# A decoder layer's SwiGLU in two phases: seven products in place of eight, and a down projection summed in PSUM

## The chip, the core and the metric

The kernel runs on one core of a Trainium2 chip. The metric is the device time of one launch in microseconds; before the change it is 1984.45 us, the median of three runs (1980.93 to 1986.12). TensorE (PE) multiplies matrices, VectorE (DVE), ScalarE (ACT) and GpSimd (POOL) do elementwise work, and SyncE (SP) issues the DMAs.

## The reference

One step of a hybrid decoder layer for 1024 prompt tokens and 8 x 8 sample tokens that share the weights: a conv branch and a sparse-attention branch, merged by gates, an output projection, and a SwiGLU FFN. The change touches the last part (D_MODEL 1024, D_FF 2816):

```python
def back(x, f, u_out, o, p):
    nsa = o.reshape(B, T, Q_W) @ p['w_nsa_o']
    mix = (f['g_conv'] * u_out + f['g_nsa'] * nsa) @ p['w_out']
    x = x + f['g1'] * mix
    h = rms_norm(x, p['ffn_norm_g']) * (1.0 + f['sc2']) + f['sh2']
    ffn = (jax.nn.silu(h @ p['w_gate']) * (h @ p['w_up'])) @ p['w_down']
    return x + f['g2'] * ffn
```

## The kernel before, in words

All is float32. A product is made of float32r matmuls: each operand is split into a high part (a copy to float32r on ScalarE, `acopy`, line 152) and a low part (source minus high, on VectorE or GpSimd), and `mm3` (lines 338 to 340) adds high x high, high x low and low x high in PSUM. `mm2` (343, 344) takes sample rows whose high and low parts lie side by side in one operand. `sub_sb` (158) alternates between VectorE and GpSimd.

Until about 1020 us the kernel computes norms, qkv, both branches and the attention; the change leaves this as it is. What follows:

- Merging (lines 1484 to 1508). For each of 8 blocks m of 128 channels and 3 chunks of tokens (`CH`: 384, 384, 320, the last with the 64 sample tokens) it loads two saved arrays from DRAM (`tn`, `mc`, five buffers), multiplies with `w_nsa_o`, and writes the merged rows as high and low parts `mh_`, `ml_`, one tile per chunk. w_out comes by 512 KB loads of 128 columns each; four of the eight run here, four later through `fr`.
- Projection (`out_half`, `norm2`). `out_half(i, j)` multiplies token tile i (eight of 128 tokens, the ninth is the samples) with half j of w_out, 24 matmuls of 512 columns, scales the sum by the gate (line 1601) and adds it to `x1[i]` (1602), which stays in SBUF. After the second half it computes the mean square and a scaled copy `xn` (1611 to 1613). `norm2` transposes `xn` on TensorE, applies the adaLN scale and shift (1580) and writes the high and low parts back into `mh_`, `ml_`, the FFN's inputs.
- FFN (`up_tile`, `down`). For each of 22 tiles of 128 of the 2816 hidden channels: 512 KB each of w_gate and w_up, split; per chunk 24 matmuls for gate and 24 for up; sigmoid and two multiplications (1663 to 1665), and the result split into `acth`, `actl`. After every second tile `down` loads two tiles of w_down, and for each token tile and half of the output sums the two tiles' products in PSUM (2 x 3 matmuls of 512 columns), scales them (1701) and adds them to `x1` (1702). The last `down` stores.

The order of instructions on every engine is set by a planner, which simulates the program and on each engine takes the ready instruction that stands first in program order; a later instruction can so be put ahead of one whose operands aren't ready. At run time each queue is in order. A tile of a pool has a fixed number of buffers (`bufs`): a new tile with the same tag waits until the oldest is released, and a pool opened after another was closed may lie in its memory and wait for its tiles.

Of the kernel before, what the change touches and what calls it, by code (L numbers as in the profile page):

```python
# [19 lines left out]
D = 1024  # L20
# [103 lines left out]
def emit(tc, I, O):  # L124
# [1345 lines left out]
    mh_ = [T(mp, [128, 8, 384], f"mh{c}", F32R) for c in range(3)]  # L1470
    ml_ = [T(mp, [128, 8, w], f"ml{c}", F32R) for c, (_, w) in enumerate(CH)]
    woS = ExitStack()
    wop = mkpool(woS, "wo", side="right")
    with ExitStack() as es:
        cp2 = mkpool(es, "c1")
        wo = [[T(wop, [128, 8, 512], f"wo{e}{j}", F32R) for e in "hl"] for j in range(2)]
        wov = I["w_out"].rearrange("(k p) c -> p k c", p=128)

        def load_wo(m, raw):

            last[0] = nc.sync.dma_start(raw, wov[:, :, m * 128:m * 128 + 128])
            hi, lo = (t[:, :, m % 4 * 128:m % 4 * 128 + 128] for t in wo[m // 4])
            acopy(hi, raw)
            (V if WOE[m] == 'V' else G).tensor_tensor(lo, raw, f(hi), op=ALU.subtract)

        for m in range(8):
# [3 lines left out]
            if m in WOM:  # L1490
                load_wo(WOM.index(m), T(cp2, [128, 8, 128], "woraw", bufs=2))
            if w_:
                two = T(pss, [128, 2, 512], "pS", bufs=2)
            for c in (1, 2, 0):
                c0, w = CH[c]
                tn = T(cp2, [128, 384], "tn", bufs=5)
                mc = T(cp2, [128, 384], "mc2", bufs=5)
                nc.sync.dma_start(tn[:, :w], th_d[8 + m][:, c0:c0 + w])
                nc.sync.dma_start(mc[:, :w], mc_d[m][:, c0:c0 + w])
                if w_:  # L1500
                    pn[m, c] = nsa(two[:, c - 1, :w] if c else T(ps, [128, 512], "pT", bufs=3)[:, :w], w_, c)
                V.scalar_tensor_tensor(tn[:, :w], tn[:, :w], 1.0, pn.pop((m, c)), op0=ALU.add, op1=ALU.mult)
                V.tensor_tensor(tn[:, :w], tn[:, :w], mc[:, :w], op=ALU.add)
                acopy(mh_[c][:, m, :w], tn[:, :w])
                n = min(w, TP - c0)
                G.tensor_tensor(ml_[c][:, m, :n], tn[:, :n], f(mh_[c][:, m, :n]), op=ALU.subtract)
                if n < w:
                    G.tensor_tensor(mh_[c][:, m, w:], tn[:, n:w], f(mh_[c][:, m, n:w]), op=ALU.subtract)
# [3 lines left out]
    gp = mkpool(top, "gp")  # L1512
    x1p = mkpool(top, "x1")
    x1 = [T(x1p, [128, D], f"x1_{i}") for i in range(9)]

    def gates(i, out, pool, tag, bufs, ps):
        gm = T(pool, [128, 8, 128], tag, bufs=bufs).rearrange("p a b -> p (a b)")[:19]
        nc.sync.dma_start(gm, g_d[i])
        for ind, n in (("indgp", 128), ("indgs", 128)):
            g_ = T(gp, [n, D], ind)  # L1520
            out.append(g_)
            for j in range(2):
                pg_ = T(ps, [128, 512], "pt", bufs=4)
                PE.matmul(pg_[:n], C(ind)[:19], gm[:, j * 512:j * 512 + 512], start=True, stop=True)
                acopy(g_[:, j * 512:j * 512 + 512], pg_[:n], 1.0 if i else 0.5)
                yield

    def load_up(t, pool):

        for nm in ("w_gate", "w_up"):  # L1530
            raw = T(fr, [128, 8, 128], "w", bufs=3)
            nc.sync.dma_start(raw, I[nm][:, t * 128:t * 128 + 128].rearrange("(k p) c -> p k c", p=128))
            first = t == 0 and nm == "w_gate"
            hi, lo = (T(fr if first else pool(), [128, 8, 128], "w" if first else f"w{e}", F32R, bufs=3) for e in "hl")
            acopy(hi, raw)
            sub_sb(lo, raw, f(hi))
            yield hi, lo


    h2h, h2l = mh_, ml_  # L1540
# [3 lines left out]
    c2S = ExitStack()  # L1544
    cp2 = mkpool(c2S, "c2")
    ssq2 = T(cp2, [128, 9], "ssq2")
    rs2 = T(cp2, [128, 9], "rs2")
    G1, G2 = [], []
    for _ in gates(0, G1, cp2, "xn", 2, psf):
        pass  # L1550

    def load_x1(i):
        n = 128 if i < 8 else 64
        nc.sync.dma_start(x1[i][:n], I["x_prompt"][i * 128:(i + 1) * 128] if i < 8 else I["x_sample"])

    for i in range(2):
        load_x1(i)
    for m in range(len(WOM), 8):
        load_wo(m, T(fr, [128, 8, 128], "w", bufs=3))
    with tc.issue_after(getattr(last[0], "ins", last[0])):  # L1560
        for i in range(2, 9):
            load_x1(i)
    G.memset(x1[8][64:128], 0.0)
    fwp = []
    ld0 = load_up(0, lambda: fwp[0])
    wgu = [next(ld0)]

    xns = {}

    def norm2(tiles):  # L1570
        c, o = tiles[0] // 3, tiles[0] % 3 * 128
        n = 64 if tiles[0] == 8 else 128
        w = n * len(tiles)
        for k in range(8):
            pt = T(psf, [128, 512], "pt", bufs=4)
            for j, i in enumerate(tiles):
                PE.transpose(pt[:, j * 128:j * 128 + n], xns[i][:n, k * 128:(k + 1) * 128], ident[:n, :n])
            hf = T(cp2, [128, 384], "hf2", bufs=2)
            if n == 128:
                V.tensor_scalar(hf[:, :w], pt[:, :w], A2[:, k, 0:1], B2[:, k, 0:1], op0=ALU.mult, op1=ALU.add)  # L1580
            else:
                hs_ = hf[:, :64].rearrange("p (b t) -> p b t", b=8)
                V.tensor_tensor(hs_, pt[:, :64].rearrange("p (b t) -> p b t", b=8), bc(A2[:, k, 1:9], 2, 8), op=ALU.mult)
                V.tensor_tensor(hs_, hs_, bc(B2[:, k, 1:9], 2, 8), op=ALU.add)
            acopy(h2h[c][:, k, o:o + w], hf[:, :w])
            sub_sb(h2l[c][:, k, o:o + w], hf[:, :w], f(h2h[c][:, k, o:o + w]))

    def out_half(i, j):
        n = 128 if i < 8 else 64
        c, o = i // 3, i % 3 * 128  # L1590
        gx = G1[i == 8]
        p = T(psf, [128, 512], "pf", bufs=4)
        for k in range(8):
            w_ = [wo[j][e][:, k, :] for e in range(2)]
            if i < 8:
                mm3(p, mh_[c][:, k, o:o + n], ml_[c][:, k, o:o + n], *w_, k == 0, k == 7)
            else:
                mm2(p, mh_[2][:, k, 256:384], *w_, k == 0, k == 7)
        tmp = T(cp2, [128, 512], "xt", bufs=2)
        xj = x1[i][:, j * 512:j * 512 + 512]  # L1600
        V.tensor_tensor(tmp, p, gx[:, j * 512:j * 512 + 512], op=ALU.mult)
        V.tensor_tensor(xj[:n], xj[:n], tmp[:n], op=ALU.add)
        if i == 8:

            lo = T(cp2, [64, 512], "xt", bufs=2)
            acopy(lo, tmp[64:128])
            V.tensor_tensor(xj[:n], xj[:n], lo, op=ALU.add)
        if j == 0:
            return
        xn = T(cp2, [128, D], "xn", bufs=2)  # L1610
        S.activation(xn[:n], x1[i][:n], AF.Square, accum_out=ssq2[:n, i:i + 1])
        rsqrt_mean(rs2[:n, i:i + 1], ssq2[:n, i:i + 1], D, 1)
        V.tensor_scalar(xn[:n], x1[i][:n], rs2[:n, i:i + 1], None, op0=ALU.mult)
        xns[i] = xn

    for i in range(3):
        out_half(i, 0)
    for tiles in ((0, 1), (2,), (3, 4), (5,), (6, 7)):
        for i in tiles:
            if i > 2:  # L1620
                out_half(i, 0)
            out_half(i, 1)
        norm2(tiles)
    for j in range(2):
        out_half(8, j)
    woS.close()


    with ExitStack() as es:
        fw = mkpool(es, "fw", side="right")  # L1630

        fwp.append(fw)
        fa = mkpool(es, "fa", side="right")
        wgu.append(next(ld0))
        norm2((8,))
        c2S.close()
        fb = mkpool(es, "fb", side="right")
        NF = FF // 128
        acts, wds = {}, {}

        def up_tile(t):
            wg, wu = wgu if t == 0 else load_up(t, lambda: fw)
            ah = T(fa, [128, TP + 128], "acth", F32R, bufs=3)
            al = T(fa, [128, TP], "actl", F32R, bufs=3)
            p = {}

            def product(j, c):
                p[j, c] = T(psf, [128, 512], "pf", bufs=4)
                fm(p[j, c][:, :CH[c][1]], (wg, wu)[j], (h2h[c], h2l[c]), 8, 0, CH[c][1])

            if t == 0:

                for c in range(2):
                    product(0, c)
            for c, (c0, w) in enumerate(CH):
                if (0, c) not in p:
                    product(0, c)
                product(1, c)
                pg_, pu_ = p[0, c], p[1, c]
                if t in (1, 2):  # L1660
                    next(g2, None)
                sg_ = T(fa, [128, 384], "sg", bufs=2)
                S.activation(sg_[:, :w], pg_[:, :w], AF.Sigmoid)  # L1663
                V.tensor_tensor(sg_[:, :w], sg_[:, :w], pg_[:, :w], op=ALU.mult)  # L1664
                V.tensor_tensor(sg_[:, :w], sg_[:, :w], pu_[:, :w], op=ALU.mult)  # L1665
                acopy(ah[:, c0:c0 + w], sg_[:, :w])
                n = min(w, TP - c0)
# [111 lines left out]
```

## Time and profile before

| | |
|---|---|
| median of three runs | 1984.45 us |
| the profiled execution | 1986.18 us |
| its span, first to last instruction | 1984.4 us |
| TensorE busy | 1901.3 us (96%) |
| VectorE busy | 1328.0 us (67%) |
| ScalarE, GpSimd busy | 716.6, 759.6 us |
| mean granted TensorE clock | 0.982 |
| DMA | 191.37 MB, 96 GB/s over the span |

Busy is the share of the span in which an engine has at least one instruction under way. A matmul's record holds its time through the array, so that records of successive matmuls overlap; how fast they follow each other is read from their starts. An idle time is put down to what ended it. The clock is in shares of full speed (2.4 GHz); 0.5 is the lower of its two levels, 1.2 GHz.

### The profile page before, as it was taken

How to read it: one execution, taken by the hardware profiler on the slowest of the kernel's cores; microseconds unless marked ns; L12 is line 12 of the kernel's file. 1: busy time of each engine (PE TensorE's matmuls, PEld its weight loads, DVE VectorE, ACT ScalarE, POOL GpSimd, SP SyncE). 2: the span in 40 equal slices, each digit the busy share in tenths (PEclk: the TensorE clock that was granted, in tenths of full speed). 3: DMA queues.
4: the chain of work that ended last, by engine and by line, in shares of the span. 5: the costliest groups of instructions: out<-in, count | busy, mean ns of one | idle time of the engine just before them, and what ended most of it. 6: DMA issues, size and time to landing. Idle time of an engine off the chain costs nothing.

```text
span 1984.4 us, 29719 instructions
## 1 busy us (share of the span) xinstructions
PE 1901.3 (96%) x11036; PEld 1707.7 (86%) x11036; DVE 1328.0 (67%) x2217; ACT 716.6 (36%) x1711; POOL 759.6 (38%) x737
## 2 busy tenths in 40 slices
PE   8987999999999699999998999999999999999998
PEld 3887998898898598888877889899999999999997
DVE  4778799969969667888865563535634644653655
ACT  5435632445444326777843233121121111112110
POOL 3888401256346475654545224121121121121213
PEclk9999999999999899999999999999999999999999
DMA  9586444445534442100036302111121111111102
GB/s 314 165 250 216 143 123 139 143 123 161 157 129 143 131 150 102 48 19 1 7 105 205 101 11 76 54 49 48 33 64 32 43 54 33 43 54 43 43 11 91
DMA packets 170823, 191.37 MB, mean 96 GB/s; under 512 B 13847, under 2 KB 135719, under 8 KB 170606
## 3 DMA queue, kind: packets, MB, share of 16 engines
q1 hardware_dynamic: 161462, 155.91, 25.5%
q0 software_dynamic: 9216, 33.56, 5.1%
q8 instruction: 87, 1.43, 0.3%
q14 instruction: 58, 0.48, 0.1%
HBM read 163.65 MB, written 30.27 MB: 98 GB/s over the span
## 4 chain that ended last, share of the span: by engine, by line
PE 55%; DVE 2%; issue 1%; DMA 1%; ACT 0%; POOL 0%; SPq 0%; DVEq 0%; POOLq 0%; ACTq 0%
PE pf L338 10%; PE pf L340 10%; PE pf L339 10%; PE pt L340 4%; PE pt L339 4%; PE pt L338 4%; PE pT L1400 3%; PE po L1407 2%; PE po L1408 2%; PE pS L1359 1%; PE pS L1361 1%; PE pS L1364 1%; DVE x L1702 0%; PE pt L343 0%; PE pt L344 0%
## 5 line engine op out<-in xcount | busy, mean ns | idle before, releaser
L338 PE MATMUL pf<-mh,wh 128*128 128x384 f32 (+1 forms) x1032 | 336.7, 326 | 0.0
L340 PE MATMUL pf<-mh,wl 128*128 128x384 f32 (+1 forms) x1032 | 336.5, 326 | 0.0
L339 PE MATMUL pf<-ml,wh 128*128 128x384 f32 (+1 forms) x1032 | 336.5, 326 | 0.0
L1668 POOL TENSOR_TENSOR actl<-sg,acth 128x384 fp32r<-128x384 f32 (+1 forms) x66 | 66.4, 1005 | 488.9 <-ACT acth L152 488.9
L338 PEld LDWEIGHTS pf<-mh,wh 128*128 128x128 f32 x1032 | 193.7, 188 | 7.3 <-DVE sg L1665 3.0
L340 PEld LDWEIGHTS pf<-mh,wl 128*128 128x128 f32 x1032 | 193.7, 188 | 4.0
L339 PEld LDWEIGHTS pf<-ml,wh 128*128 128x128 f32 x1032 | 193.7, 188 | 3.2
L338 PE MATMUL pd<-hh,whi 128*128 128x384 f32 (+1 forms) x576 | 193.5, 336 | 1.0 <-ACT stg L152 0.9
L340 PE MATMUL pd<-hh,wlo 128*128 128x384 f32 (+1 forms) x576 | 191.6, 333 | 0.8 <-DVE wlo L270 0.8
L339 PE MATMUL pd<-hl,whi 128*128 128x384 f32 (+1 forms) x576 | 191.5, 332 | 0.0
L1096 DVE SCALAR_TENSOR_TENSOR y<-U,wdT,y 128x1024 f32<-128x1024 f32 x120 | 161.9, 1349 | 0.6
L1702 DVE TENSOR_TENSOR x<-x,dt 128x512 f32<-128x512 f32 x180 | 146.3, 813 | 5.4
L340 PE MATMUL pt<-wdh,actl 128*128 128x512 f32 x352 | 139.0, 395 | 0.0
L339 PE MATMUL pt<-wdl,acth 128*128 128x512 f32 x352 | 138.5, 393 | 0.0
L1663 ACT ACTIVATE sg<-pf 128x384 f32<-128x384 f32 (+1 forms) x66 | 30.8, 467 | 295.1 <-PE pf L340 291.8
L338 PE MATMUL pt<-wdh,acth 128*128 128x512 f32 x352 | 137.1, 389 | 0.0
L1664 DVE TENSOR_TENSOR sg<-sg,pf 128x384 f32<-128x384 f32 (+1 forms) x66 | 34.9, 528 | 146.4 <-ACT sg L1663 146.4
L1701 DVE TENSOR_TENSOR dt<-pt,indgp 128x512 f32<-128x512 f32 x160 | 110.7, 692 | 25.9 <-PE pt L340 10.9
L958 POOL TENSOR_TENSOR vv<-kraw,vv 128x256 fp32r<-128x256 f32 x80 | 92.0, 1175 | 66.1 <-ACT vv L152 65.9
L338 PEld LDWEIGHTS pd<-hh,whi 128*128 128x128 f32 x576 | 109.6, 190 | 7.7 <-ACT stg L152 1.2
L1388 POOL TENSOR_SCALAR P<-P,ast 128x640 f32<-128x640 f32 (+7 forms) x128 | 89.1, 723 | 70.0 <-DVE ast L1384 68.1
L152 ACT ACTIVATE whi<-wraw 128x512 fp32r<-128x512 f32 (+1 forms) x133 | 81.7, 626 | 92.4 <-PE pd L339 41.2
(493 smaller groups left out, 4920.5 us busy)
## 6 DMA issues: line engine op xcount, KB each, us to landing
wraw<-in_w_in SPq DMA_DIRECT2D x68, 256.0 KB
wraw<-in_w_ada SPq DMA_DIRECT2D x64, 256.0 KB
w<-in_w_gate SPq DMA_DIRECT2D x22, 512.0 KB
w<-in_w_up SPq DMA_DIRECT2D x22, 512.0 KB
w<-in_w_down SPq DMA_DIRECT2D x22, 512.0 KB
x<-in_x_prompt SPq DMA_DIRECT2D x16, 512.0 KB
araw<-in_w_ada SPq DMA_DIRECT2D x32, 256.0 KB
th_d<-th SPq DMA_DIRECT2D x32, 192.0 KB
```

What stands on the lines that cost most here:

```text
L152: S.activation(out, in_, AF.Copy, scale=scale)
L338: PE.matmul(out, ah, bh, start=first, stop=False)
L339: PE.matmul(out, ah, bl, start=False, stop=False)
L340: PE.matmul(out, al, bh, start=False, stop=last)
L958: G.tensor_tensor(vv[:, :, 1], r, f(vv[:, :, 0]), op=ALU.subtract)
L1096: V.scalar_tensor_tensor(op, U[:, k:k + TP], wk, op, op0=ALU.mult, op1=ALU.add)
L1388: G.tensor_scalar(P_[br][g][:, :w], P_[br][g][:, :w], st[:, 2, br, g:g + 1], 1.0, op0=ALU.mult, op1=ALU.mult)
L1400: PE.transpose(pT[:nk, g * 128:(g + 1) * 128], a, ident)
L1407: PE.matmul(po, va, ph[:nk], start=(bi == 0), stop=False)
L1668: G.tensor_tensor(al[:, c0:c0 + n], sg_[:, :n], f(ah[:, c0:c0 + n]), op=ALU.subtract)
L1701: V.tensor_tensor(tmp, p, gx[:, cs_], op=ALU.mult)
L1702: (G if last and j == 0 else V).tensor_tensor(x1[i][:, cs_], x1[i][:, cs_], tmp, op=ALU.add)
```

## The change

**Gate and up** are seen as one product of 2 x 2 blocks: rows gate and up, inner dimension in two halves (a) of 512 channels, and columns in two token segments (r). Strassen's scheme (in Winograd's form) makes it of seven block products in place of eight. There are two token groups u, each of two segments: 256 + 256 tokens, and 288 + 288 (256 prompt and 32 sample tokens each). Every merged or normed row lies in `qh[a][segment]`, `ql[a][segment]`. `norm2` now works on a segment; `build(u)` makes the four sums of input blocks and splits them (32 VectorE and 16 ScalarE instructions on 512 columns for both groups, and for u = 1 those of the sample columns). `load_up(t)` loads four blocks of the weights, splits three, and makes and splits the four weight sums: 14 tiles, each with a single buffer, six in the pool `aw0`, eight in `aw1`. The pool `aw1`, and `st` for the sums, are opened after `x1`'s pool is closed, behind `build(1)`.

**Activations** of each tile and group are stored in DRAM (`act_d`). **Down** is a second phase: per half j of the output and group u it accumulates all 22 tiles in PSUM, one bank per token tile (and one for the samples); activations are loaded and split again, w_down once per half. The first 17 tiles run tile by tile, the last five token tile by token tile, each then scaled, added to x1 from DRAM and stored. The operand memory of the first phase holds the second's (`ring`, `wpl`).

**Projection.** `x1` is kept in halves: each is stored to DRAM (`x1_d`) after its sum. All nine first halves run first, then the second ones with their norms. The scaled rows of tiles 4 to 7 go to buffers of earlier first halves, the others' are made in place. w_out is loaded in rows of 512 columns, 256 KB each. The gate rows of the FFN (`gates(1)`) come behind the first pass of the second phase.

The core of the diff:

```diff
+            for sg in range(4):          # merging: cut at segment bounds
+                lo_, hi_ = max(c0, 256 * sg), min(c0 + w, TP, 256 * sg + 256)
...
+                acopy(qh[a][sg][:, r, d], tn[:, e])
+                G.tensor_tensor(ql[a][sg][:, r, d], tn[:, e], f(qh[a][sg][:, r, d]), op=ALU.subtract)
...
+    def build(u):
+        views = [([t[a] for t in full[u]], [[t[:, 2 * a:2 * a + 2, :256] for t in x] for x in tb[u]]) for a in range(2)]
...
+        for (b11, b21, b12, b22), dst in views:
+            V.tensor_tensor(b11, b12, b11, op=ALU.subtract)
+            V.tensor_tensor(b12, b22, b12, op=ALU.subtract)
+            V.tensor_tensor(b22, b22, b11, op=ALU.subtract)
+            V.tensor_tensor(b21, b21, b22, op=ALU.subtract)
+            for src, j in ((b22, 1), (b12, 2), (b11, 0), (b21, 3)):
+                acopy(dst[j][0], src)
+                V.tensor_tensor(dst[j][1], src, f(dst[j][0]), op=ALU.subtract)
+    for i in range(9):
         out_half(i, 0)
+    for sg in (0, 1):
+        for i in (2 * sg, 2 * sg + 1):
             out_half(i, 1)
+        norm2(sg)
+    build(0)
+    out_half(8, 1)
...
+    def load_up(t):
...
+        split(1, a11, V)
+        split(2, a12, V)
+        V.tensor_tensor(s1, a21, a22, op=ALU.add)
+        V.tensor_tensor(a21, a11, a21, op=ALU.subtract)
+        split(7, a21, V)
+        V.tensor_tensor(a11, s1, a11, op=ALU.subtract)
+        yield op
+        if len(ap_) < 2:
+            build(1)
+            xS2.close()
+            ap_.append(mkpool(uS, "aw1"))
+            stg.append(mkpool(uS, "st"))
+        split(6, a11, V)
+        V.tensor_tensor(a12, a12, a11, op=ALU.subtract)
+        split(5, s1, G)
+        split(3, a12, V)
+        split(4, a22, G)
+        yield op
...
+    up0 = load_up(0)
+    for sg in (2, 3):
+        if sg == 3:
+            next(up0)
+        for i in (2 * sg, 2 * sg + 1):
+            out_half(i, 1)
+        norm2(sg)
+        if sg == 2:
+            norm2s()
...
+    for t in range(NF):
...
+        for u in range(2):
+            def product(p):
+                out = T(psf, [128, 512], "pf" if p in (1, 7, 2, 4) else "pt", bufs=4)[:, :w]
+                bh, bl = right(p, u)
+                for k in range(4):
+                    mm3(out, op[p][0][:, k], op[p][1][:, k], bh[:, k, :w], bl[:, k, :w], k == 0, k == 3)
+                return out
...
+            acopy(c11, product(1))
+            add(c12, product(6), c11)
+            add(c21, product(7), c12)
+            p5 = product(5)
...
+            nc.sync.dma_start(act_d[u][t], g)
...
+        LATE = 5
+        for j in range(2):
+            for u in range(2):
+                pd_ = {4 * u + n: T(psf, [128, 512], ("pf", "pt")[u], bufs=4) for n in range(4)}
...
+                for t in range(NF):
+                    if u == 0:
+                        load_down(j, t)
+                    a = load_act(u, t)
+                    if t >= NF - LATE:
+                        late.append((t, a))
+                        continue
+                    for i in order:
+                        step(i, t, a)
+                if not G2:
+                    G2 += gates(1, dn)
+                for i in order:
+                    for t, a in late:
+                        step(i, t, a)
...
```

## Rows read from the trace of the kernel before

**Rows 1.** The page, part 1: engines, busy us, share of the span, instructions
```profile
PE 1901.3 (96%) x11036; PEld 1707.7 (86%) x11036; DVE 1328.0 (67%) x2217; ACT 716.6 (36%) x1711; POOL 759.6 (38%) x737
```

**Rows 2.** The page, part 4: the chain that ended last, by engine, by line
```profile
PE 55%; DVE 2%; issue 1%; DMA 1%; ACT 0%; POOL 0%; SPq 0%; DVEq 0%; POOLq 0%; ACTq 0%
PE pf L338 10%; PE pf L340 10%; PE pf L339 10%; PE pt L340 4%; PE pt L339 4%; PE pt L338 4%; PE pT L1400 3%; PE po L1407 2%; PE po L1408 2%; PE pS L1359 1%; PE pS L1361 1%; PE pS L1364 1%; DVE x L1702 0%; PE pt L343 0%; PE pt L344 0%
```

**Rows 3.** Windows: stretch, length, busy us (instructions) by engine, PEclk, DMA share, GB/s
```profile
200.00:300.00 100.00, 97.63 (x587) 91.10 (x587) 86.06 (x185) 49.81 (x176) 27.03 (x19) 0.96 0.43 129
...
1040.00:1060.00 20.00, 16.52 (x79) 15.90 (x80) 14.91 (x22) 8.88 (x14) 12.02 (x12) 0.83 1.01 301
...
1100.00:1200.00 100.00, 100.00 (x494) 84.80 (x493) 62.23 (x116) 32.37 (x68) 25.01 (x31) 1.00 0.13 35
...
1333.80:1405.30 71.50, 71.50 (x395) 66.99 (x394) 36.79 (x51) 11.82 (x18) 14.17 (x11) 1.00 0.15 46
```

**Rows 4.** Timeline of TensorE in the FFN: start, us, engine, line, operation
```profile
1303.10 0.31 PE L338 MATMUL pf<-mh,wh 128*128 128x320 f32 x1
...
1309.99 0.31 PE L340 MATMUL pf<-mh,wl 128*128 128x320 f32 x1
...
1326.80 0.31 PE L338 MATMUL pf<-mh,wh 128*128 128x320 f32 x1
...
1333.83 0.39 PE L338 MATMUL pt<-wdh,acth 128*128 128x512 f32 x1
...
1339.08 0.39 PE L340 MATMUL pt<-wdh,actl 128*128 128x512 f32 x1
...
1905.35 0.39 PE L338 MATMUL pt<-wdh,acth 128*128 128x512 f32 x1
```

**Rows 5.** The chain in order of time, 1010 to 1095 us: start, us, what
```profile
1036.05 6.86 DMA woraw<-in_w_out
```

**Rows 6.** Timeline of TensorE in the qkv stage
```profile
161.81 0.28 PE L339 MATMUL pz<-wlo,hh 128*128 128x256 f32 x1
...
165.89 0.28 PE L340 MATMUL pz<-whi,hl 128*128 128x256 f32 x1
```

**Rows 7.** VectorE's groups: line, operation, names, shapes, count, busy us, mean ns, idle
```profile
L1664 DVE TENSOR_TENSOR sg<-sg,pf 128x384 f32<-128x384 f32 x44 | 24.3, 551 | 138.6 <-ACT sg L1663 138.5
...
L1580 DVE TENSOR_SCALAR hf<-pt,A,B 128x256 f32<-128x256 f32 x24 | 12.5, 541 | 5.9 <-PE pt L1577 3.8 <-POOL ml L158 1.4
...
L1602 DVE TENSOR_TENSOR x<-x,xt 128x512 f32<-128x512 f32 x16 | 11.3, 708 | 0.4
...
L1601 DVE TENSOR_TENSOR xt<-pf,indgp 128x512 f32<-128x512 f32 x16 | 11.0, 687 | 12.5 <-PE pf L340 12.4
...
L1664 DVE TENSOR_TENSOR sg<-sg,pf 128x320 f32<-128x320 f32 x22 | 10.6, 482 | 7.8 <-ACT sg L1663 7.8
...
L158 DVE TENSOR_TENSOR ml<-hf,mh 128x256 fp32r<-128x256 f32 x12 | 7.1, 588 | 1.5 <-ACT mh L152 1.3
```

**Rows 8.** ScalarE's groups, the same columns
```profile
L152 ACT ACTIVATE whi<-wraw 128x512 fp32r<-128x512 f32 x132 | 81.3, 628 | 81.7 <-PE pd L339 41.2 <-DMA wraw<-in_w_ada 15.8 <-DMA wraw<-in_w_in 13.2
```

**Rows 9.** Timeline of VectorE and GpSimd near the end
```profile
1959.56 0.69 DVE L1702 TENSOR_TENSOR x<-x,w 128x512 f32<-128x512 f32 x1
...
1971.98 1.30 POOL L1702 TENSOR_TENSOR x<-x,w 128x512 f32<-128x512 f32 x1 [1.23 <-DVE w L1701]
...
1972.54 1.29 DVE L1702 TENSOR_TENSOR x<-x,w 128x512 f32<-128x512 f32 x1
```

**Rows 10.** GpSimd's groups, the columns of Rows 7
```profile
L1506 POOL TENSOR_TENSOR ml<-tn,mh 128x384 fp32r<-128x384 f32 x16 | 18.0, 1139 | 15.4 <-ACT mh L152 15.4
...
L158 POOL TENSOR_TENSOR ml<-hf,mh 128x256 fp32r<-128x256 f32 x12 | 11.0, 920 | 28.6 <-ACT mh L152 28.6
```

**Rows 11.** Timeline of TensorE after the gate matmuls
```profile
1090.13 0.63 PE L338 MATMUL pf<-woh,mh 128*128 128x512 f32 x1
...
1092.69 0.55 PE L338 MATMUL pf<-woh,mh 128*128 128x512 f32 x1
```

More of the change, by code (lines that the diff above doesn't have):

```diff
@@ L1503, in emit @@
                 V.tensor_tensor(tn[:, :w], tn[:, :w], mc[:, :w], op=ALU.add)
[L1504 to L1508, printed above, removed]
+                a, r = m // 4, m % 4
+                for sg in range(4):
+                    lo_, hi_ = max(c0, 256 * sg), min(c0 + w, TP, 256 * sg + 256)
+                    if lo_ >= hi_:
+                        continue
+                    d, e = (slice(lo_ - 256 * sg, hi_ - 256 * sg), slice(lo_ - c0, hi_ - c0))
+                    acopy(qh[a][sg][:, r, d], tn[:, e])
+                    G.tensor_tensor(ql[a][sg][:, r, d], tn[:, e], f(qh[a][sg][:, r, d]), op=ALU.subtract)
+                if c == 2:
+                    acopy(ms[:, m, 0:64], tn[:, 256:320])
+                    G.tensor_tensor(ms[:, m, 64:128], tn[:, 256:320], f(ms[:, m, 0:64]), op=ALU.subtract)
     pbS.close()
     hS.close()
[L1512 to L1540, printed above, removed]
     psS_ = ExitStack()
@@ new lines, in emit, with gates @@
+    xS2 = ExitStack()
+    xp1 = mkpool(xS2, "x1")
+    cp2 = mkpool(xS2, "c2")
+    x1_d = T(dp, [9, 128, D], "x1_d")
+    act_d = [T(dp, [FF // 128, 128, 2, SEG[2 * u]], f"act_d{u}") for u in range(2)]
+    def gates(i, pool):
+        out = [T(pool, [128, D], ind, bufs=1) for ind in ("indgp", "indgs")]
+        for j in range(2):
+            gm = T(pool, [128, 512], "xt", bufs=3)
+            nc.sync.dma_start(gm[:19], g_d[i][:, j * 512:j * 512 + 512])
+            for ind, g_ in zip(("indgp", "indgs"), out):
+                pg_ = T(psf, [128, 512], "pt", bufs=4)
+                PE.matmul(pg_, C(ind)[:19], gm[:19], start=True, stop=True)
+                acopy(g_[:, j * 512:j * 512 + 512], pg_, 1.0 if i else 0.5)
+        return out
@@ L1560, in emit @@
+    for k in range(8):
+        load_wo(1, k, T(fr, [128, 512], "w", bufs=6))
     with tc.issue_after(getattr(last[0], "ins", last[0])):
         for i in range(2, 9):
[L1562 to L1586, printed above, removed]
@@ new lines, in emit, with place @@
+    full = [[None] * 4, [None] * 4]
+    tb = [None, None]
+    def place(sg):
+        u, r = sg // 2, sg % 2
+        if r == 0:
+            tb[u] = [[quarter(u) for _ in range(2)] for _ in range(4)]
+        for a in range(2):
+            if sg == 0:
+                full[u][a] = [T(ap_[0], [128, 2, 256], "aw", bufs=6) for _ in range(2)]
+            else:
+                x = T(mp, [128, 4, SEG[1 + r * u * 2]], ("qh0", "ql0")[a] + str(1 + r * u * 2))
+                full[u][2 * r + a] = [x[:, 2 * b:2 * b + 2, :256] for b in range(2)]
```

318 lines of the change are left out of this document (191 added, 127 removed).

## The prediction

> **What bounds the kernel now.** I read the busy table first: TensorE is busy 96% of the span [rows 1]. The chain that ended last says the same in another way: 55% of it is TensorE, and its largest lines are the three matmul lines of `mm3` (338 to 340) with output `pf` and then `pt`, which in the last 40% of the time are the FFN [rows 2]. Then the windows: from 1100 us on TensorE is at 100% at a granted clock of 1.00, VectorE at 62% and 51% [rows 3]. "Busy" there is a model, since a matmul record lasts longer than the distance to the next one, so I took the price of a matmul from starts, not durations. In one FFN tile a run of 48 matmuls of 320 columns starts at 1303.10 and its last one at 1309.99: 6.89 / 47 = 0.1466 us each. The same run of the next tile starts at 1326.80, so a tile's gate and up take 23.70 us, and the 96 matmuls of 384 columns in it (23.70 - 48 x 0.1466) / 96 = 0.1736 us each. The down matmuls of a pair of tiles start at 1333.83 and, eight pairs on, at 1905.35: a pair takes 71.44 us, its down part 71.44 - 2 x 23.70 = 24.04 us, or 0.2312 us for each of 104 [rows 4]. No start in these runs waits for anything: the FFN is bound by the number of columns streamed. The stretch before it (1020 to 1077 us, merging the branches) is not: TensorE has little to do there, the clock falls to 0.83 and the DMA engines stand at 301 GB/s [rows 3]; the chain goes through a w_out load that took 6.86 us [rows 5].
>
> **The products (gain).** Gate and up of a tile were 48 matmuls in each of three token chunks (384, 384, 320). They become 7 products of 4 x 3 = 12 matmuls in each of two token groups: 84 of 256 columns and 84 of 288. A 256-column matmul with a weight load each, of the same type, is in the qkv stage: starts 161.81 to 165.89 hold 34 steps, 0.1200 us each [rows 6], which lies on the line through 320 and 384 columns (0.1196). 288 columns lie halfway to 320: 0.1333. So 84 x 0.1200 + 84 x 0.1333 = 21.28 us in place of 23.70, and 22 x 2.42 = 53.2 us go. An eighth of the columns is saved; 24 more matmuls a tile, at some 0.012 us each whatever the width, take a little of it back.
>
> **The down matmuls (small gain).** 22 x 52 = 1144 of 512 columns before and after. Their mean is 0.2312 us, but the undisturbed 24 that open a pair run at (1339.08 - 1333.83) / 23 = 0.2283 [rows 4]. Long accumulations could run at that: between 0 and -3.3 us; I take -2. The 160 and more VectorE additions into x1 that go cost nothing now (VectorE is half idle there [rows 3]), so they give nothing.
>
> **The VectorE side of the products.** Per tile VectorE gets 5 splits and 4 weight sums of 512 columns (0.708 us, as line 1602 [rows 7]) = 6.4 us, and per token group 11 additions and multiplications: line 1664 takes 0.551 at 384 and 0.482 at 320 columns [rows 7], so 0.448 at 288 and 0.414 at 256: 9.5 us. Sum 15.9 of 21.28 us. ScalarE: 7 copies of 0.628 [rows 8], 2 copies and 4 sigmoids at about 0.4 = 6.8 us. Both fit. But the operand tiles are single: a weight operand is free after its product of the second token group and wanted 6/14 of a tile later, 9.1 us, in which its ScalarE copy and VectorE subtract must come up in queues that also hold product sums. From 200 to 300 us VectorE is at 86% and TensorE still at 97.6% [rows 3]. So a friction of 8 us over the 22 tiles, with 0 and 62 as ends (the second rival).
> The trace adds to this: line 1702 on VectorE takes 0.69 us alone and 1.29 us when GpSimd has its own two-operand instruction running (1971.98 for 1.30, VectorE's from 1972.54) [rows 9]. It ends 0.55 us after GpSimd's: it waited, and was not merely slowed. The Trainium skill (SBUF — State Buffer, Who interferes with whom) says that a VectorE instruction with two SBUF inputs fully blocks while GpSimd reads SBUF. This speaks against the change, which puts two GpSimd subtracts of 512 columns in each tile; the trace agrees. By the trace alone they can block VectorE 2 x 1.3 = 2.6 us a tile: 18.5 us, still under 21.28.
>
> **Between the projection and the first product (loss).** Now this stretch is a continuous run of TensorE: out_half, transposes and the first tile are interleaved. In the new order all nine first halves come first, then the nine second halves with their norms, and VectorE's work crowds into the latter. From [rows 7]: 9 x (0.687 + 0.708) for the sums, about 1 us per tile for scaling and the mean, 16 x 0.541 for `hf`, 12 x 0.588 for the low parts (the other half of them is on GpSimd at 0.920 [rows 10]), 2.3 for the sample rows, `build` twice with 16 x 0.70 plus 2.4 for the sample's, 6 x 0.70 for the first weight operands: 12.6 + 9 + 8.7 + 7.1 + 2.3 + 24.8 + 4.2 = 69 us. It can't start before the second tile's second half is done, 48 x 0.228 = 11 us in: it ends at 80 us or later. TensorE has 208 matmuls x 0.228 + 72 transposes = 55 us there. Products 1, 7 and 2 of the first group (36 x 0.12 = 4.3 us) have their operands early; the others wait for a pool that lies where x1 lay, and stand behind `build(1)` in VectorE's queue. So 80 - 55 - 4 = 21 us idle, taken as 22 with the copies in between; ends 5 (the planner puts the first operands ahead of `build(1)`) and 40 (VectorE blocked by GpSimd as above). After such a stop the clock is at half: after the gate matmuls at 1086 us seven matmuls of 512 columns were 0.427 apart in place of 0.23 [rows 11], 7 x 0.2 = 1.4 us. That is added.
>
> **The merge stretch.** w_out's first half comes in 2 KB rows in place of 512 B ones, and x1 in halves: in a stretch where the DMA engines are full this may save some of the 6.86 us load [rows 5]. Against it the merged rows are cut at segment bounds: 6 copies and 6 to 7 GpSimd subtracts per m in place of 3 and 4, at 1.139 for 384 and 0.920 for 256 columns [rows 10], about 1 us of GpSimd more per m, and these release the five `tn` buffers. -8 to +8; I take 0.
>
> **The second phase.** All activations go to DRAM and come back, each once per half of w_down. In the first group of each half a tile needs two loads of 256 KB in 12 x 0.228 = 2.74 us: 191 GB/s, below the 301 shown [rows 3]; its two copies (1.26 us) and subtracts (1.4 us) fit as well. Free tiles of the last product tile let the first loads run ahead, and the second group's run during the late five tiles. 3 us for the two starts and the gate matmuls, which are now in one block and pull the clock down once; ends 0 and 24. The end is alike: last sum, scale, add, one store.
>
> **Sum.** From the profiled execution (1986.2 us, 1.8 above its span, 0.09% above the median): 1986.2 - 53.2 - 2 + 22 + 1.4 + 8 + 0 + 3 = 1965.4; for the median 1.7 less: 1964.
>
> **Rivals.**
> First: the planner hides the transition. For it: in the trace of before the first tile's matmuls stand between the transposes and nothing idles. Against it: there the operands were ready. Then 5 in place of 22, 2 of friction, -3 in the merge, 0 in the second phase: 1964 - 17 - 6 - 3 - 3 = 1935.
> Second, the slower side: VectorE becomes the bound of the products. If its two-input SBUF instructions wait as in [rows 9]: 9 x 1.29 + 8 x 0.80 + 14 x 0.43 = 24.0 us a tile. It decides from 21.28 us on; then 22 x 2.8 = 62 us in place of 8: 2018. For it: the in-order queues and single operands. Against it: GpSimd is at work only an eighth of the tile.
> Third: the second phase waits for its loads. At 160 GB/s a tile of the first group takes 3.28 us in place of 2.74, 44 x 0.54 = 24 us in place of 3: 1985, no change. That the change doesn't do what it says would be 256-column matmuls held at 0.17 us by their weight loads; [rows 6] exclude it.
>
> **Chances.** Forecast 0.50, first rival 0.22, second 0.13, third 0.15. A measurement of this kernel can't tell less than 0.3% (6 us) from no change. Faster by more: nearly all of the first two and a quarter of the third, 0.73; within: 0.13; slower: 0.14, the second rival and bad sums of the others. Range: 1933 to 2000, which leaves out most of the second rival and little else. The forecast's own range is 1945 to 1982.
>
> **What would show it.** Right: starts 0.120 and 0.133 us apart in the products, 21.3 to 22 us a tile; one idle stretch of TensorE of 15 to 30 us, ended by VectorE, before the first full tile; down starts at 0.228 to 0.231. Wrong: TensorE waits in every tile for VectorE's or ScalarE's splits (second rival), or for loads in the second phase (third), or no idle stretch at all (first).

## The result and the profile after

The kernel after takes 1940.72 us (median of 4 runs, 1937.66 to 1943.51), the kernel before beside it 1983.69 us (4 runs); the ratio is 0.9766, 95% interval 0.9745 to 0.9787. So 43 us went, and 20 were forecast: faster, as predicted, inside the range, but by more than twice the forecast gain. The profiled execution took 1940.07 us (before 1986.18), its span is 1938.3.

The page of the kernel after, parts 1 and 4, answers to [rows 1, 2]:

```profile
PE 1852.7 (96%) x11564; PEld 1660.0 (86%) x11564; DVE 1390.5 (72%) x2567; ACT 842.5 (43%) x2049; POOL 661.4 (34%) x656
...
PE 53%; DVE 3%; POOL 1%; issue 1%; ACT 1%; DMA 0%; DVEq 0%; POOLq 0%; ACTq 0%
```

TensorE is still the bound, with 49 us less of it. Windows of the kernel after (columns as in [rows 3]): the merge, the projection, the transition to the FFN, ten tiles of products, the down phase.

```profile
1040.00:1060.00 20.00, 16.48 (x84) 15.71 (x83) 12.86 (x22) 8.22 (x23) 15.03 (x20) 0.83 0.95 302
1100.00:1180.00 80.00, 80.00 (x366) 65.60 (x365) 37.49 (x69) 24.99 (x59) 8.99 (x11) 1.00 0.15 52
1180.00:1217.00 37.00, 26.18 (x151) 23.04 (x149) 34.15 (x69) 25.01 (x57) 15.41 (x12) 0.72 0.22 71
1380.40:1590.40 210.00, 210.00 (x1682) 210.00 (x1682) 153.16 (x310) 67.22 (x130) 29.10 (x20) 1.00 0.25 78
1720.00:1930.00 210.00, 210.00 (x918) 172.08 (x917) 81.17 (x152) 58.41 (x120) 0.00 (x0) 1.00 0.45 135
```

Only the third is new: TensorE stands for 29% of it (26.18 of 37 us busy) while VectorE is busy for 34.15 of 37 us, and the mean clock is 0.72. In the other FFN windows TensorE is full at 1.00.

TensorE's timeline in one tile (start first) gives the price of a product: the first matmuls of a group of 84 with 288 columns, of the 84 with 256, and of the next group.

```profile
1382.57 0.29 PE L338 MATMUL pf<-qh,aw 128*128 128x288 f32 x1
...
1393.77 0.28 PE L338 MATMUL pf<-qh,aw 128*128 128x256 f32 x1
...
1403.57 0.29 PE L338 MATMUL pf<-qh,aw 128*128 128x288 f32 x1
```

11.20 / 84 = 0.1333 us and 9.80 / 84 = 0.1167 us: a tile takes 21.00 us (before 23.70 [rows 4]), and TensorE waits nowhere in it. The difference of the two profiled executions is read stretch by stretch between four marks: last `po` matmul of the attention, first matmul of out_half, last product, last matmul. First those of the kernel before (its products end with its down part), then those of the kernel after:

```profile
1023.49 0.39 PE L1408 MATMUL po<-pl,vhl 128*128 128x512 f32 x1
...
1077.11 0.50 PE L338 MATMUL pf<-woh,mh 128*128 128x512 f32 x1 [1.56 <-DVE tn L1502]
...
1976.47 0.39 PE L340 MATMUL pt<-wdh,actl 128*128 128x512 f32 x1
```

```profile
1026.35 0.39 PE L1408 MATMUL po<-pl,vhl 128*128 128x512 f32 x1
...
1075.68 0.50 PE L338 MATMUL pf<-tq,qh 128*128 128x512 f32 x1 [1.89 <-DVE tn L1516]
...
1666.64 0.30 PE L340 MATMUL pf<-tq,aw 128*128 128x288 f32 x1
...
1933.37 0.39 PE L340 MATMUL pt<-qh,tq 128*128 128x512 f32 x1
```

The marks are read to 0.1 us. Before, products and down alternate; their lengths are 22 x 23.70 and 11 x 24.04, the gate matmuls (eight records) stand between them (4.2 us, counted under down, as after), and what remains is the transition.

| stretch, us | before | after | change | forecast |
|---|---|---|---|---|
| to the end of the attention | 1023.5 | 1026.3 | +2.8 | 0 |
| merge, to out_half | 53.6 | 49.4 | -4.2 | 0 |
| out_half, transition | 109.4 | 128.9 | +19.5 | +23.4 |
| products | 521.4 | 462.0 | -59.4 | -45.2 |
| down, gates | 268.6 | 266.7 | -1.9 | +1 |
| last matmul's start to the end | 7.9 | 4.9 | -3.0 | 0 |

The first line is code that the change leaves alone. In the traces of all kernels here that stretch ended between 1021.7 and 1033.4 us, so a single time can't carry 3 us, and below each effect is read from its own stretch. "Transition" there is the time from the first out_half matmul to the last product's start less 22 tiles at that kernel's tile length: 128.9 us in the kernel after.

### The profile page after: what moved, and what is told of

The parts are those of the page before. It is cut to its first block, busy times and chain, and to the rows that moved or that the text cites. A ratio compares the mean times of both kernels' runs of the same rounds, so it can differ in the third digit from the quotient of the medians.

```text
span 1938.3 us, 32279 instructions
## 1 busy us (share of the span) xinstructions
PE 1852.7 (96%) x11564; PEld 1660.0 (86%) x11564; DVE 1390.5 (72%) x2567; ACT 842.5 (43%) x2049; POOL 661.4 (34%) x656
## 4 chain that ended last, share of the span: by engine, by line
PE 53%; DVE 3%; POOL 1%; issue 1%; ACT 1%; DMA 0%; DVEq 0%; POOLq 0%; ACTq 0%
PE pf L338 8%; PE pf L339 8%; PE pf L340 8%; PE pt L338 5%; PE pt L339 5%; PE pt L340 5%; PE pT L1400 3%; PE po L1407 2%; PE po L1408 2%; PE pS L1359 1%; PE pS L1361 1%; PE pf L344 1%; PE pf L343 1%; POOL ql L1525 1%; PE pS L1364 1%
## 5 line engine op out<-in xcount | busy, mean ns | idle before, releaser
L1705 POOL TENSOR_TENSOR aw<-s,aw 128x512 fp32r<-128x512 f32 x21 | 27.3, 1300 | 302.0 <-ACT aw L152 286.5
L152 ACT ACTIVATE aw<-w 128x512 fp32r<-128x512 f32 x133 | 83.0, 628 | 92.5 <-PE pf L339 62.9
L338 PEld LDWEIGHTS pd<-hh,whi 128*128 128x128 f32 x576 | 109.4, 190 | 7.8 <-ACT stg L152 1.2
L1404 DVE TENSOR_TENSOR pl<-pT,ph 128x512 fp32r<-128x512 f32 (+1 forms) x148 | 99.3, 681 | 19.2 <-ACT ph L152 17.9
L340 PEld LDWEIGHTS pd<-hh,wlo 128*128 128x128 f32 x576 | 109.2, 190 | 3.9 <-DVE wlo L270 2.2
L339 PEld LDWEIGHTS pd<-hl,whi 128*128 128x128 f32 x576 | 109.2, 190 | 2.9 <-issue 0.5
L338 PE MATMUL pz<-whi,hh 128*128 128x256 f32 (+1 forms) x320 | 94.5, 297 | 12.0 <-ACT zt L152 10.2
L338 PE MATMUL pt<-tq,aw 128*128 128x256 f32 (+1 forms) x352 | 101.9, 290 | 2.1 <-ACT aw L152 2.1
L339 PE MATMUL pt<-tq,aw 128*128 128x256 f32 (+1 forms) x352 | 102.2, 290 | 1.6 <-DVE tq L1671 1.6
L338 PE MATMUL pf<-tq,aw 128*128 128x256 f32 (+1 forms) x352 | 101.9, 289 | 1.7 <-ACT aw L152 1.7
L339 PE MATMUL pf<-tq,aw 128*128 128x256 f32 (+1 forms) x352 | 101.8, 289 | 0.0
L339 PE MATMUL pf<-ql,aw 128*128 128x256 f32 (+1 forms) x352 | 101.8, 289 | 0.0
L340 PE MATMUL pf<-tq,aw 128*128 128x256 f32 (+1 forms) x352 | 101.7, 289 | 0.0
L340 PE MATMUL pf<-qh,aw 128*128 128x256 f32 (+1 forms) x352 | 101.7, 289 | 0.0
L338 PE MATMUL pf<-qh,aw 128*128 128x256 f32 (+1 forms) x352 | 101.6, 289 | 0.0
```

What stands on the lines that cost most here:

```text
L152: S.activation(out, in_, AF.Copy, scale=scale)
L338: PE.matmul(out, ah, bh, start=first, stop=False)
L339: PE.matmul(out, ah, bl, start=False, stop=False)
L340: PE.matmul(out, al, bh, start=False, stop=last)
L1404: V.tensor_tensor(pl_[:nk], pT[:nk], f(ph[:nk]), op=ALU.subtract)
L1705: e.tensor_tensor(lo, src, f(hi), op=ALU.subtract)
```

## The experiments

**The two phases without the seven products.** Eight block products for each tile and group, no sums; the rest as after, but for the place where `norm2` puts its rows.

```diff
-            acopy(c11, product(1))
-            add(c12, product(6), c11)
...
+            for r in range(2):
+                c1, c2 = product(1, r, "pf"), product(3, r, "pt")
+                S.activation(g[:, r], c1, AF.Sigmoid)
```

> The changed kernel with eight block products in place of seven: gate and up are summed over both halves of the inner dimension in PSUM, so the sums of input blocks, of weight blocks and of products are left out; the two phases, the pools and the projection's order stay. Theory (the gain is the eighth of the columns, priced by the steps between starts): a tile takes 96 x 0.1167 + 96 x 0.1333 = 24.0 us in place of 21.0, 22 x 3.0 = 66 us more; the idle stretch before the first product goes with the sums, 15 to 19 us less: 1987 to 1992 us, that is level with the kernel before or a little slower. Rival (the two phases, with long sums in PSUM and no sums on VectorE, bring a good part of the 43 us themselves): 1955 to 1975 us.

1990.51 us, ratio 1.0016 (1.0003 to 1.0028). ScalarE's timeline has the sigmoids of successive tiles 24.00 us apart, which is 96 x 0.1167 + 96 x 0.1333:

```profile
1301.71 0.39 ACT L1748 ACTIVATE g<-pf 128x288 f32<-128x288 f32 x1
...
1325.71 0.39 ACT L1748 ACTIVATE g<-pf 128x288 f32<-128x288 f32 x1
```

The transition is 115.0 us, 13.9 less than after; but 3.3 us of these are waits in the last tile (27.26 us long, all others but the first 24.00), so ahead of the full tiles 17.2 us are gone with the sums. The theory came out in its numbers, and the rival fell: the new form with eight products is no faster than the kernel before. The profiled executions of this kernel and of the kernel after lie 47.2 us apart: 22 x 3.00 = 66.0 us of products more, 17.2 less without the sums, 3.3 more in the last tile, and 4.9 less in all other stretches.

**How much VectorE can take.** VectorE does its subtract of each weight split twice, then three times:

```diff
-            e.tensor_tensor(lo, src, f(hi), op=ALU.subtract)
+            for _ in range(2 if e is V else 1):
+                e.tensor_tensor(lo, src, f(hi), op=ALU.subtract)
```

> The changed kernel with each VectorE subtract of a weight split in the products done twice (the second time with the same result): 5 x 0.6 = 3.0 us more VectorE work per tile, 18.4 of 21.0 us. Theory (the planner keeps VectorE's work beside TensorE as long as it fits; friction is nil until VectorE itself is full): tile 21.0 to 21.2 us, 1941 to 1946 us with three more subtracts before the first tile. Rival (friction in the queues grows with VectorE's load, as the 8 us of the prediction assumed at 15.9 us): half of what is added comes out, tile 22 to 22.5 us, 1963 to 1975 us.

> The same with three subtracts for one: 6.0 us more, 21.4 us of VectorE per tile against 21.0 of TensorE. Theory (max of the two engines): VectorE becomes the bound, with GpSimd's two subtracts of 1.3 us in its way a tile takes 21.6 to 23 us, 1955 to 1990 us; TensorE then waits for splits. Rival (friction grows with the load): tile 24 us and over, 2005 us or more.

Twice: 1946.76 us, ratio 0.9802 (0.9778 to 0.9826). Three times: 1958.57, ratio 0.9867 (0.9847 to 0.9887). The windows from 1300 to 1600 us, first of the one, then of the other, and TensorE's waits there in the second (us in all, times, longest); the first has none.

```profile
1300.00:1600.00 300.00, 300.00 (x2405) 300.00 (x2404) 262.19 (x516) 91.92 (x184) 38.38 (x28) 1.00 0.25 78
```

```profile
1300.00:1600.00 300.00, 293.80 (x2328) 292.02 (x2327) 291.92 (x570) 87.31 (x180) 61.23 (x27) 1.00 0.24 75
...
PE pt L338 <- ACT aw L152: 6.0, 7, 1.6
```

With VectorE at 87% a tile is still 21.0 us and TensorE never waits; at 97% the waits come, 2% of the time, and a tile takes 21.7 us in the mean. The first run lost 5.7 us (transition 134.6) ahead of its third tile: 3.8 of them in the second tile (24.84 us), where TensorE waits for splits on GpSimd and VectorE. In the steady tiles in-order queues and single operand buffers cost nothing at 73% and 87%: the second rival fell, and with it the 8 us of friction.

**The order in the transition.** Held behind: the first tile's later splits, on ScalarE and GpSimd as well as on VectorE, may not be issued before the last instruction of `build(1)`, the order which the prediction assumed. Ahead: `build(1)` is written behind these splits.

```diff
+        with tc.issue_after(getattr(end, "ins", end)) if t == 0 else ExitStack():
+            split(6, a11, V)
...
```

```diff
-            build(1)
             xS2.close()
...
         split(4, a22, G)
+        if t == 0:
+            build(1)
```

> The changed kernel, but VectorE's subtracts for operands 6, 3 of the first tile (and the weight sum between them) are held in VectorE's queue behind the last instruction of build(1), which is what the prediction took for granted. Theory (the idle stretch was 8 us shorter than predicted because the planner put these splits ahead of the sums of the second group): the first tile starts 8 to 12 us later, 1948 to 1953 us. Rival (the stretch is set by VectorE's total, whatever the order): 0 to 2 us, 1940 to 1943 us.

> The kernel after, with the sums of the second token group (build(1)) written behind all splits of the first tile's weights, where the kernel after has them ahead of the second half of the splits. It is the opposite of the run with the splits held behind, which cost 10.1 us between the start of out_half and the products. Theory (the transition's length is set by what stands on VectorE ahead of the first tile's operands): the first token group's seven products, 9.8 us of TensorE, no longer wait for build(1)'s 12 us, which then run beside them; the products' effective start comes 3 to 7 us earlier than the 128.9 us after the start of out_half, and the ratio to the kernel before is 0.973 to 0.975. Rival (it is VectorE's total work in the stretch that sets the length, whatever its order, since the second group then waits for build(1) in the place of the first): 127 to 131 us, ratio 0.976 to 0.978.

Behind: 1947.30 us, ratio 0.9796 (0.9774 to 0.9818), transition 139.0, 10.1 more than after. Ahead: 1938.15, ratio 0.9744 (0.9720 to 0.9767), transition 127.9. The first theory's 8 to 12 us came out in its stretch. The second theory's ratio came out, but the interval holds the rival's too, and the transition, one trace of each, lies where the rival had it. TensorE's timeline of the first shows the two stops, which the kernel after doesn't have:

```profile
1208.58 0.58 PE L338 MATMUL pt<-tq,aw 128*128 128x256 f32 x1 [8.65 <-ACT aw L152]
...
1212.84 0.58 PE L340 MATMUL pt<-tq,aw 128*128 128x256 f32 x1 [3.47 <-POOL aw L1706]
```

VectorE's timeline of the kernel after shows why writing the splits ahead brings nothing more: the planner already put two of them (L1705) before the rest of `build(1)` (L1667 to 1671).

```profile
1205.03 0.68 DVE L1705 TENSOR_TENSOR aw<-w,aw 128x512 fp32r<-128x512 f32 x1
...
1207.80 1.77 DVE L1705 TENSOR_TENSOR aw<-w,aw 128x512 fp32r<-128x512 f32 x1
1209.49 1.78 DVE L1667 TENSOR_TENSOR ql<-ql,qh 128x512 f32<-128x512 f32 x1
...
1219.01 0.69 DVE L1671 TENSOR_TENSOR tq<-ql,tq 128x512 fp32r<-128x512 f32 x1
```

With the order forced that the prediction assumed, TensorE's waits from 1176 to 1218 us add up to 20.2 us (3.5 of them for a split on GpSimd), and 22 were forecast; in the kernel after, to 11.2. So the idle time was sized about right for that order, and the order was misjudged. But the forced stretch is 29.6 us longer than before and not the 23.4 of the forecast: the sum of the transition was short by 6.2 us even then.

**Three more tries at the transition.** Scale and shift of the second group on ScalarE (with the splits ahead); the evictions of the last two token tiles written ahead of `build(0)` (with the splits ahead, 5 and 4 on VectorE); scaled rows in place for all tiles.

```diff
-            if k % 2:
+            if k % 2 or u:
```

```diff
-    build(0)
     out_half(8, 1)
...
+        if sg == 3:
+            build(0)
+            next(up0)
         norm2(sg)
```

```diff
-            xn = T(xp1, [128, 512], "x10", bufs=9) if 3 < i < 8 else x1[i, a]
+            xn = x1[i, a]
```

> The same, and the adaLN scale and shift of the prompt rows of the second token group (16 instructions of norm2, half of them on VectorE) all on ScalarE: VectorE loses 8 x 0.45 us, ScalarE gets as much. Theory (VectorE's work is what bounds the transition): another 2 to 4 us earlier than the run before it. Rival (order alone counts, or ScalarE takes VectorE's place): no difference from it within 1.5 us, or later.

> Three changes of order to the kernel after, to shorten the transition: the sums of the first token group (build(0)) are written behind the second halves of the last two token tiles, so that their evictions stand ahead of build(0)'s 7.5 us of VectorE (in the kernel after, TensorE's last out_half matmul starts at 1180.0 and its sum is scaled at 1189.0 only); build(1) is written behind the first tile's splits; and splits 5 and 4 are on VectorE. Theory (the transition is a chain: eviction, mean square, scaling, transposes, operands; it is the place in VectorE's queue that lengthens it): the products' effective start is 119 to 124 us after the start of out_half in place of 128.9, the ratio 0.971 to 0.974, the fastest version. Rival (the work in VectorE's queue sets the length; what is put ahead holds build(0) and with it products 7, 6 and 5 back by as much): 126 to 131 us, ratio 0.975 to 0.978.

> The changed kernel with the scaled rows of tiles 4 to 7 made in place, as those of the other tiles. Theory (these writes then wait until the row's store to DRAM has read it, some 2.5 us, in the stretch where VectorE and ScalarE hold TensorE up): 1 to 4 us slower, 1942 to 1945 us. Rival (the stores are done by then, or other work fills the wait): no difference, 1940 to 1941 us.

They took 1937.02 (ratio 0.9746, 0.9725 to 0.9767), 1939.34 (0.9765, 0.9737 to 0.9794) and 1936.72 us (0.9758, 0.9736 to 0.9780), with transitions of 127.1, 128.6 and 130.3 us. No transition differs by over 2 us from that of the kernel after, and the rivals hold, with two exceptions: with rows in place the stretch is 1.4 us longer, as the theory had it, though the time doesn't show it; and the theory of the second was not put to the test, as said below. TensorE's waits of the kernel after from 1178 to 1222 us, then those of the run with rows in place, whose stop moved into one place:

```profile
PE pt L1634 <- ACT x L152: 5.0, 3, 2.3
PE pt L338 <- ACT aw L152: 2.1, 2, 1.2
PE pf L338 <- ACT aw L152: 1.7, 1, 1.7
PE pt L339 <- DVE tq L1671: 1.6, 2, 1.1
```

```profile
PE pt L1634 <- ACT x L152: 9.5, 3, 7.6
PE pf L338 <- ACT aw L152: 1.7, 1, 1.7
```

And VectorE's waits with the scale and shift on ScalarE: it gives up eight instructions, some 4.2 us, and waits 3.6 us for ScalarE instead.

```profile
DVE ql L158 <- ACT qh L152: 1.7, 2, 1.0
...
DVE qh L1665 <- ACT qh L1637: 1.2, 2, 1.0
DVE qh L1666 <- ACT ql L1637: 0.7, 2, 0.5
```

In the run with the evictions first the planner gave VectorE almost the order of the kernel after (the last tile's eviction, 1185.16, again behind `build(0)`), so the theory's order itself was not tried. None of these versions can be told from the kernel after. Which link holds the transition at about 127 us stays open.

**GpSimd beside VectorE.** Splits 5 and 4 on VectorE.

```diff
-        split(5, s1, G)
+        split(5, s1, V)
...
-        split(4, a22, G)
+        split(4, a22, V)
```

> The kernel after with the two weight splits that GpSimd does in each tile (5 and 4) on VectorE, so that in the tiles no GpSimd instruction runs beside VectorE's. Theory (a tile is bound by TensorE's columns; GpSimd blocking VectorE costs nothing there): a tile stays at 21.0 us, TensorE without waits; line 1723 on VectorE falls from 1.74 to 0.69 us; the time as the kernel after, ratio 0.975 to 0.979. Rival (the blocking costs some tenths in each tile, or moved work delays operands): a tile other than 21.0 by more than 0.1, 2 us or more in all.

1938.70 us, ratio 0.9753 (0.9733 to 0.9773), a tile 21.00 us. The group of line 1723 from 1300 to 1600 us (columns as in [rows 7]), after and here:

```profile
L1723 DVE TENSOR_TENSOR w<-w,w 128x512 f32<-128x512 f32 x15 | 26.1, 1743 | 0.0
```

```profile
L1723 DVE TENSOR_TENSOR w<-w,w 128x512 f32<-128x512 f32 x14 | 9.5, 680 | 0.0
```

GpSimd holds that VectorE instruction up by 1.06 us in each tile, as [rows 9] and the Trainium skill (SBUF — State Buffer, Who interferes with whom) had it. In the tiles it costs no time, since VectorE has 5.7 us to spare in each. The transition was 126.5, 2.4 less than after; one trace can't say whether that comes of GpSimd.

**The gate rows.** Before the first product in place of the second phase, kept in DRAM:

```diff
+    gates_store()
...
-                    G2 += gates(1, dn)
+                    for n in range(2):
+                        G2.append(T(dn, [128, D], f"g2{n}", bufs=1))
+                        nc.sync.dma_start(G2[n], g2_d[n])
```

> The changed kernel with the FFN's gate rows made before the first product, where TensorE idles, stored to DRAM and loaded back in the second phase, in place of behind its first pass. Theory (there the four fp32 matmuls take 3.9 us of TensorE's own time and leave it at half clock for 1.6 us more): 4 to 6 us faster than the changed kernel, 1935 to 1937 us, without the half-clock run behind the first pass. Rival (the idle stretch is bound by VectorE and ScalarE, and four more ScalarE copies there lengthen it by as much): 0 to -2 us, 1938 to 1941 us.

1944.96 us, ratio 0.9787 (0.9763 to 0.9811). The down phase is 5.3 us shorter, as the block in the kernel after lets one expect: four gate matmuls (eight records), then matmuls of 512 columns 0.43 us apart before they return to 0.23 (TensorE's timeline).

```profile
1713.12 3.69 PE L1552 MATMUL pt<-xt,ck 19*128 19x512 f32 x8
...
1717.75 0.63 PE L338 MATMUL pf<-tq,qh 128*128 128x512 f32 x1
1718.18 0.63 PE L339 MATMUL pf<-tq,qh 128*128 128x512 f32 x1
...
1720.72 0.39 PE L339 MATMUL pf<-tq,tq 128*128 128x512 f32 x1
```

But the transition is 137.7, 8.8 longer: the gate matmuls weren't put into TensorE's stops but stood ahead of products that were due, one block of them after a wait for its own load, and the products behind ran at half clock (256 columns 0.213 us apart). The theory missed. The rival was right that the time can't be had there, but not in its size (0 to 2 us faster; the ratio is 0.0021 above that of the kernel after, some 4 us) and not in its reason, ScalarE's copies.

```profile
1205.73 0.41 PE L339 MATMUL pf<-tq,aw 128*128 128x256 f32 x1
1209.17 3.75 PE L1564 MATMUL pt<-xt,ck 19*128 19x512 f32 x4 [3.03 <-DMA xt<-g_d]
```

**The kernel before with w_out in 2 KB rows:**

```diff
-            last[0] = nc.sync.dma_start(raw, wov[:, :, m * 128:m * 128 + 128])
+            last[0] = nc.sync.dma_start(raw, I["w_out"][k * 128:k * 128 + 128, j * 512:j * 512 + 512])
```

> The kernel before, with only w_out's loads as in the change: 256 KB each in rows of 512 columns (2 KB) in place of 512 KB in rows of 128 columns. Theory (the merge became 4 us shorter because these loads no longer hold the DMA engines and the w_out copies up): 3 to 5 us faster than the kernel before, 1978 to 1981 us, the projection starts 3 to 5 us earlier against the end of the attention. Rival (it is the cut merged rows and the smaller x1 loads): 0 to -1 us.

1983.78 us, ratio 0.9989 (0.9971 to 1.0008): inconclusive in time. The merge took 49.7 us in place of 53.6; the kernel after has 49.4. The stretch agrees with the theory. The run that follows, with the old loads, took 52.2 us, and the eleven traces of the kernel after and its variants 46.3 to 49.4, so loads in longer rows seem to bring some 2.5 to 4 us of this stretch; the total doesn't show it.

**The kernel before with the last additions on VectorE:**

```diff
-                    (G if last and j == 0 else V).tensor_tensor(x1[i][:, cs_], x1[i][:, cs_], tmp, op=ALU.add)
+                    V.tensor_tensor(x1[i][:, cs_], x1[i][:, cs_], tmp, op=ALU.add)
```

> The kernel before with the additions of the last down step all on VectorE, where every second one was on GpSimd; nothing else differs. Theory (the 3 us by which the kernel after ends sooner behind its last matmul come from the two engines no longer blocking each other): the span ends 4.7 to 6 us after TensorE's last matmul in place of 7.7. Rival (they come from the stores, nine of which stand in the queue there, or from the output rows' order): 7 to 8 us, as before.

One run. The span ended at 1990.0; its last matmul and last addition in the timelines, then the last additions of the kernel before:

```profile
1984.54 0.39 PE L340 MATMUL pt<-wdh,actl 128*128 128x512 f32 x1
...
1986.13 0.69 DVE L1702 TENSOR_TENSOR x<-x,w 128x512 f32<-128x512 f32 x1
```

```profile
1977.03 1.26 POOL L1702 TENSOR_TENSOR x<-x,w 128x512 f32<-128x512 f32 x1 [1.23 <-DVE w L1701]
1977.69 1.16 DVE L1702 TENSOR_TENSOR x<-x,w 128x512 f32<-128x512 f32 x1
```

From the last matmul's start to the end it is 5.5 us, before 7.9, after 4.9 (counted so, all are some 0.2 to 0.4 above the marks of the expectation); the run with w_out in 2 KB rows, which ends like the kernel before, has 7.9 too. So 2.4 of the 3.0 us go with GpSimd's additions, as the theory's number said. But the blocking of VectorE isn't the reason: the last addition ends 2.3 us behind the last matmul's start here (1986.82) and 2.4 before (1978.85). The time lies behind it. GpSimd closes the program with a DRAIN, an instruction of its sequencer that stands behind its last work; it is the longest of three (shortest, median and longest in ns, then the first and last start). Before, here, and in the kernel after:

```profile
L1775 POOLq DRAIN  x3: 45/102/6618, 1977.0 to 1984.1; - x3
```

```profile
L1775 POOLq DRAIN  x3: 45/102/6377, 1962.4 to 1989.7; - x3
```

```profile
L1918 POOLq DRAIN  x3: 45/102/6645, 1647.4 to 1938.0; - x3
```

The long DRAIN is the first of the three, and in all 14 traces it ends 5.3 us after GpSimd's last instruction. Before, that is at 1977.0 + 6.6 = 1983.6, and the program ends 0.8 us later, while SyncE, behind its last store, had been done by 1981.4. Here and in the kernel after it was over long before the end.

## Why the prediction was right in direction and too small

The forecast for the profiled execution was 1965.4, the result 1940.07: 25.3 us apart. By its own steps:

- **The products: right in kind, 6.2 us too small.** 288 columns take 0.1333 us, as interpolated. 256 take 0.1167 and not the 0.1200 of [rows 6], so a tile takes 21.00 us in place of 21.28: 22 x 0.28 = 6.2 us. The clock was 1.00 in both stretches, in that of [rows 6] by the window in the last section; why the same form runs slower in that part of the qkv stage stays open. The line through 320 and 384 columns gave 0.1196 and hid it.
- **"A friction of 8 us over the 22 tiles": the step that failed, the largest single error.** No steady tile showed any. The step argued from single operand buffers and from [rows 3], where TensorE is at 97.6% beside a VectorE at 86%; but that is another stage with its own loads, and here 87% left TensorE at 100%. VectorE's load itself was well sized: 15.9 us in a tile forecast, 15.3 measured (153.16 / 10). The second rival let all its two-input instructions wait for GpSimd; one in a tile does (its 62 us were 22 x 2.72 = 60 by its own numbers).
- **"The others ... stand behind `build(1)` in VectorE's queue": failed, 3.9 us net.** The planner put the operands of the first products ahead, which the prediction held only for the range's end: TensorE waits 11.2 us in place of 22, and the forced order shows that this is worth 10.1 us. The other 6.2 go the other way. The half clock was undersized: 1.4 us for seven matmuls, read behind gate matmuls and not behind a stop, where 37 matmuls of 256 columns ran 0.1 us late each (3.6) and 14 transposes too (1.4). Waits and clock make 16.2 of the stretch's 19.5 us. Another 2.6 lie in the 11 stops themselves: the profile counts a wait from the end of a matmul's record (0.28 us long at 256 columns), while in a run without waits the next matmul starts 0.117 us after that one's start.
- **The merge, taken as 0: -4.2 us.** The bound was -8 to +8. The run with w_out's rows points to the loads for most of it.
- **"The end is alike": failed, 3.0 us.** Sum, scaling, addition and store are alike, within 0.6 us. What the step left out is the DRAIN of GpSimd, whose last work moved from the end of the program to the end of the products.
- **The down matmuls and the second phase: 2.9 us too dear.** +1 forecast, -1.9 measured (265.1 to 268.4 us in the variants that share this code, before 268.6). TensorE is full at 1.00 there, no load is waited for, and the third rival fell.

With the attention's 2.8 us the other way these make up the 25.3. The first rival's 1935 came nearer than the forecast, by its price and not by its picture: the transition wasn't hidden.

## What to carry to other kernels

Cut columns from the bound engine and charge the helpers nothing in the steady state until they are really full: here VectorE at 87% cost a steady tile nothing, and at 97% TensorE waited 2% of the time. Before a step is charged for standing behind another in a queue, ask whether a planner is free to put it ahead; one run with the order forced tells the price. What a saving costs shows up at the change of phase, where the clock falls too, and it is to be read there, not from the total. Let GpSimd finish some microseconds before the program does: its closing DRAIN held the end of the kernel before.

## What was not expected of the hardware

The same float32r matmul of 256 columns follows its neighbour in 0.1200 us in one steady run [rows 6] and in 0.1167 in another, both at a granted clock of 1.00. The window of the first (columns as in [rows 3]):

```profile
161.80:166.00 4.20, 4.20 (x37) 4.20 (x36) 4.20 (x10) 0.26 (x2) 3.43 (x4) 1.00 0.68 174
```

A block of four gate matmuls (eight records) that occupies TensorE for 3.6 us without a gap can leave the clock at half for the matmuls behind it, 0.43 us apart for 512 columns, though TensorE never stopped. Of the ten kernels with this block in the second phase eight show it; the one with eight products and the one with three subtracts don't (a clock of 1.00 from 1762 to 1775 us in the first, whose block starts at 1761.9). In the kernel before the same matmuls come in four pairs between 1218 and 1246 us, and the clock stays at 1.00:

```profile
1762.00:1775.00 13.00, 13.00 (x50) 9.13 (x51) 3.46 (x5) 2.82 (x5) 0.00 (x0) 1.00 0.21 69
```

```profile
1210.00:1260.00 50.00, 50.00 (x284) 46.02 (x283) 8.75 (x14) 13.86 (x23) 13.89 (x11) 1.00 0.29 85
```

And GpSimd's closing DRAIN ends 5.3 us after its last instruction, whether that stands at the end of the program or 730 us before it.
